# Loading rows 52 to 62 of each partition in six transfers instead of eight

## The chip, the cores and the metric

The kernel runs on one core of a Trainium2 chip. The metric is the time of one execution on the device in microseconds (us), less being better; runs of one kernel agree within about 0.2 us here. The core has a matrix engine (PE, TensorE), three engines for elementwise work and reductions (DVE is VectorE, ACT is ScalarE, POOL is GpSimd), a synchronizing engine (SP), and 16 DMA engines that move data between the device memory and the on-chip memory. On-chip memory has 128 partitions. PE writes its results into a separate accumulator memory, from which DVE or ACT must copy them before PE can read them as an operand.

## What is computed

A router: 16 x 512 = 8192 rows of 1024 numbers are multiplied by a 1024 x 8 weight matrix, and a softmax is taken over the 8 results of each row.

```python
def reference(x, router_weights):          # x: 16 x 512 x 1024, router_weights: 1024 x 8, float32
    logits = np.matmul(x, router_weights)
    exp_logits = np.exp(logits - np.max(logits, axis=-1, keepdims=True))
    return (exp_logits / np.sum(exp_logits, axis=-1, keepdims=True)).astype(np.float32)
```

The input is 33.6 MB, and the output only 0.26 MB.

## The kernel before

Each of the 128 partitions holds 64 of the 8192 rows, and "row j" below means row j of every partition: 128 rows of the input, 512 KB in the device memory. The whole input is kept on chip in bf16 (`x_all`, `xa` in the code), which is 256 KB for a row.

**The stream.** Rows 0 to 3 come first, as float32 in two transfers that SP issues (into `x_f32`), and ACT casts them. All other rows are loaded by POOL's queue, converted to bf16 by the transfer itself. The list `LOADS` (L40) says how many rows each transfer holds, from the first four rows on: thirteen entries of 4 (rows 0 to 51), three of 2 (52 to 57), five of 1 (58 to 62). Row 63, the last, comes in three pieces of its columns (`PIECES`, of 4, 2 and 2 blocks of 128 columns). POOL issues all of them at the start (L174 and L187), and they run one after the other. Every load has a semaphore of its own (`s_ld[i]`, `s_z[i]` for the pieces).

**How rows are released.** SP waits for each load in turn (L162) and then adds the load's number of rows to one semaphore, `s_in`. PE takes 1 from it ahead of each row (L218). So a row is released only when the whole transfer that it belongs to has landed. The pieces of row 63 are waited for by PE itself (L312).

**What is done for a row.** PE transposes the row's eight 128 x 128 blocks (`loop_turn`, L282): five into one accumulator bank (`ptv`), three into another (`pts`). DVE copies the five to `xTv` (L403), ACT the three to `xTs` (L355). Then PE multiplies the eight copied blocks by the weights (`multiply`, L269 in the trace), which gives the 8 logits of the 128 rows in `lg`. Banks and copies exist twice, for even and odd rows.

**PE's order.** A loop of two rows per trip: turn of the odd row, product of the even row before it, turn of the next even row, two filler matmuls on constant data (`spare<-filler`), product of the odd row. The last trip ends with the turn of row 62. Behind the loop PE waits for the copies of row 61 (its bank is used again), and then does: the transposes of the first piece of row 63 (L315, into `pts`), the product of row 61 (L261), the transposes of the two other pieces (into `ptv` and `extra`), the product of row 62, and the product of row 63 (L329).

**The softmax** is done for groups of 8 rows: on DVE maximum (`mx`), difference (`ex`), sum, reciprocal and scaling (`out_all`), and on ACT the exponential (`ev`, L344). The groups are rows 0 to 3 with an unused half, 4 to 11, and so on; the last is 52 to 59. Inside the loops of DVE and ACT its steps stand between the copies of the rows that follow. The last four rows, 60 to 63, are done with a maximum (`low`, L454) and an exponential (L348) each, and a common sum and scaling at the very end (L507 to L511).

**The order behind the loops**, which the last group of the softmax shares with the last rows, is written out:

- DVE: copy of row 60; maximum and difference of the group 52 to 59; copy of row 61; sum of the group; maximum of row 60; reciprocal of the group; copy of row 62; maximum of row 61; copies of the second and third piece (L460); maximum of rows 62 and 63; scaling of the group; sum, reciprocal and scaling of rows 60 to 63.
- ACT: copy of row 60; exponential of the group; copy of row 61; exponential of row 60; copy of row 62; copy of the first piece (L385); exponentials of rows 61, 62 and 63.

**Stores.** SP issues two: one for the groups up to row 51 (L165), after the first piece of row 63 has landed, and one for the rest (L167), after the last scaling.

Of the kernel before, what the change touches and what calls it, by code (L numbers as in the profile page):

```python
# [11 lines left out]
def kernel(  # L12
# [24 lines left out]

    LOADS = [4] * 13 + [2, 2, 2] + [1] * 5  # L40
    PIECES = [4, 2, 2]
    G, SKIP = 8, 4
    TRIPS = 31
# [5 lines left out]
    DONE = ends[-2]  # L49
    assert sum(LOADS) == J - 1 and sum(PIECES) == KO and ends[-1] == J - ALONE  # L50

# [6 lines left out]
    def sb(name, shape, dtype):  # L58
        size = mybir.dt.size(dtype)
        for n in shape[1:]:  # L60
            size *= n
        at = place[0]
        place[0] = -(-(at + size) // 64) * 64
        return nc.alloc_sbuf_tensor_at(name, shape, dtype, offset=at).ap()
# [5 lines left out]
    xa = sb("x_all", [P, J, D], bf16)  # L70
    x_f32 = sb("x_f32", [P, LOADS[0], D], fp32)
    identity = sb("identity", [P, P], bf16)
# [33 lines left out]
    s_w = nc.alloc_semaphore("s_w")  # L106
    s_ld = [sem(f"s_ld{i}") for i in range(len(LOADS))]
    s_z = [sem(f"s_z{i}") for i in range(len(PIECES))]
# [22 lines left out]

    first = [sum(LOADS[:i]) for i in range(len(LOADS))]
    cols = [sum(PIECES[:i]) for i in range(len(PIECES))]
# [21 lines left out]

    for j in range(LOADS[0]):
        sp.wait_ge(s_cast, j + 1)
        sp.sem_inc(s_in, 1)
    for i, r in enumerate(LOADS):
        if i:  # L160
# [383 lines left out]
```

## Time and profile before

| What | Value |
|---|---|
| Median of 4 runs | 86.60 us (86.49 to 86.69) |
| The profiled execution | 86.54 us |
| Its span, from the first to the last instruction | 85.08 us |
| Busy: PE, DVE, ACT, POOL | 62.6, 39.5, 37.9, 13.4 us |
| Granted clock of PE, mean (1 is full) | 0.987 |
| Input loads on POOL's queue, share of the 16 DMA engines over the span | 90.5% |
| Device memory read | 33.59 MB, 398 GB/s over the span |
| Issue of the last load by POOL | ends at 16.7 us |

The page shows the span in 40 slices of 2.1 us. The digits are tenths of a slice in which the engine was busy.

```profile
PE   0054859999495977949596895949597799999760
DVE  0021412684374442845265362736357257665662
ACT  0039683564253352535245262525336246545470
...
DMA  2999999898989999999999999999999999999920
```

The DMA engines are busy from the second slice to nearly the last, and PE has gaps until the last ten slices. In the timelines a line gives the start and the length in us, the engine, the line of the kernel, the operation and its tile (result <- operands), the number of instructions merged into it, and in brackets how long the engine sat idle before it and what ended that. "PEq L218" is PE's wait for a released row.

### The profile page before, as it was taken

Reading aid. Unit: us, or ns where it says so; the run is one execution under the profiler, and the core shown is the slowest. Engines: PE = TensorE matmul, PEld = TensorE weight load, DVE = VectorE, ACT = ScalarE, POOL = GpSimd, SP = SyncE. Lnnn points to the kernel's source line nnn. Section 1 sums busy time; section 2 is a strip of 40 time slices with the busy share of each in tenths; the row PEclk is TensorE's granted clock in tenths of the full one; section 3 lists DMA queues with packets and bytes.
Section 4 is the critical chain, followed back from the end, with each engine's and each line's share of the span. In section 5 each row is a group of like instructions: output and inputs, shape, how many; then the busy total and the mean of one; then the engine's idle time right before and its main releaser. Section 6 shows DMA issues by size and latency. Waiting matters only on the chain. (4 is left out here: it accounts for less than half of the span.)

```text
span 85.1 us, 2942 instructions
## 1 busy us (share of the span) xinstructions
PE 62.6 (74%) x1094; PEld 51.4 (60%) x1094; DVE 39.5 (46%) x114; ACT 37.9 (45%) x81; POOL 13.4 (16%) x30
## 2 busy tenths in 40 slices
PE   0054859999495977949596895949597799999760
PEld 0042748888374765838474673837476588777650
DVE  0021412684374442845265362736357257665662
ACT  0039683564253352535245262525336246545470
POOL 0489999800000000000000000000000000000000
PEclk9999999999999999999999999999999999999995
DMA  2999999898989999999999999999999999999920
GB/s 39 362 428 308 231 189 243 189 243 189 243 189 239 193 239 193 239 193 239 193 239 193 239 193 239 193 239 193 239 193 212 216 212 212 200 212 208 190 103 23
DMA packets 3904, 18.12 MB, mean 213 GB/s; under 512 B 568, under 2 KB 1080, under 8 KB 2112
## 3 DMA queue, kind: packets, MB, share of 16 engines
q0 software_dynamic: 3312, 15.73, 90.5%
q1 hardware_dynamic: 576, 2.36, 7.1%
q10 hardware_dynamic: 16, 0.03, 0.2%
HBM read 33.59 MB, written 0.26 MB: 398 GB/s over the span
## 5 line engine op out<-in xcount | busy, mean ns | idle before, releaser
L355 ACT COPY xTs<-pts 128x384 bf16<-128x384 bf16 x63 | 30.0, 476 | 37.4 <-PE pts L282 37.1
L403 DVE COPY xTv<-ptv 128x640 bf16<-128x640 bf16 x63 | 31.0, 492 | 32.9 <-PE ptv L282 30.4
L282 PE MATMUL ptv<-identity,x_all 128*128 128x128 bf16 x311 | 28.3, 222 | 13.7 <-PEq L218 12.4
L282 PEld LDWEIGHTS ptv<-identity,x_all 128*128 (+1 forms) x311 | 18.5, 98 | 15.1 <-issue 15.0
L282 PE MATMUL pts<-identity,x_all 128*128 128x128 bf16 x186 | 21.1, 224 | 0.0
L269 PEld LDWEIGHTS lg<-w_bf,xTv 128*128 128x128 bf16 x305 | 15.5, 97 | 7.4 <-issue 0.6
L269 PE MATMUL spare<-filler 128*128 128x512 bf16 x61 | 19.0, 393 | 0.4
L269 PE MATMUL lg<-w_bf,xTv 128*128 128x8 bf16 x305 | 16.6, 167 | 0.0
L282 PEld LDWEIGHTS pts<-identity,x_all 128*128 x186 | 13.4, 100 | 0.0
L269 PE MATMUL lg<-w_bf,xTs 128*128 128x8 bf16 x183 | 13.2, 166 | 0.0
L174 POOL DMA_DIRECT2D x_all<-in_x_dram x20 | 10.7, 607 | 2.8 <-POOLq L151 2.8
L269 PEld LDWEIGHTS lg<-w_bf,xTs 128*128 128x128 bf16 x183 | 8.9, 96 | 0.0
L269 PEld LDWEIGHTS spare<-filler 128*128 128x128 bf16 x61 | 4.3, 99 | 2.5 <-issue 2.5
L276 PE MATMUL lg<-ident,w 8*128 8x8 f32 x8 | 1.0, 251 | 5.3 <-PEq L274 5.3
L276 PEld LDWEIGHTS lg<-ident,w 8*128 8x128 f32 x8 | 0.9, 198 | 5.3 <-issue 5.3
L341 ACT CAST x_all<-x_f 128x1024 bf16<-128x1024 f32 x4 | 4.0, 1044 | 0.0
L423 DVE TENSOR_REDUCE mx<-lg 128x8 f32 x8 | 1.8, 225 | 4.4 <-DVEq L473 3.9
L341 ACT ACT_TABLE_LOAD x1 | 1.3, 1283 | 5.5 <-ACTq L339 5.5
L392 DVE CAST identity<-ident 128x128 bf16<-128x128 f32 x1 | 0.5, 518 | 5.2 <-POOL ident L180 5.2
L344 ACT ACTIVATE ev<-ex 128x64 f32<-128x64 f32 x8 | 2.0, 256 | 1.6 <-DVE ex L423 0.9
L439 DVE TENSOR_REDUCE ssum<-ev 128x8 f32<-128x64 f32 x8 | 1.8, 220 | 0.1
L187 POOL DMA_DIRECT2D x_all<-in_x_dram x3 | 1.7, 697 | 0.0
(41 smaller groups left out, 16.0 us busy)
## 6 DMA issues: line engine op xcount, KB each, us to landing
x_all<-in_x_dram POOLq DMA_DIRECT2D x12, 1024.0 KB, 32.1
x_f<-in_x_dram SPq DMA_DIRECT2D x2, 1024.0 KB, 6.3
x_all<-in_x_dram POOLq DMA_DIRECT2D x3, 512.0 KB, 59.9
x_all<-in_x_dram POOLq DMA_DIRECT2D x5, 256.0 KB, 64.1
out_dram<-out_all SPq DMA_DIRECT2D x1, 208.0 KB, 1.9
x_all<-in_x_dram POOLq DMA_DIRECT2D x1, 128.0 KB, 65.7
x_all<-in_x_dram POOLq DMA_DIRECT2D x2, 64.0 KB, 65.4
out_dram<-out_all SPq DMA_DIRECT2D x1, 48.0 KB, 1.5
```

The costliest lines, as they stand in the source:

```text
L174: nc.gpsimd.dma_start(out=xa[:, first[i]:first[i] + r, :], in_=x_rows[:, first[i]:first[i] + r, :]).then_inc(s_ld[i], 16)
L187: nc.gpsimd.dma_start(out=xa[:, J - 1, c], in_=x_rows[:, J - 1, c]).then_inc(s_z[i], 16)
L269: return pe.matmul(spare, lhsT=filler[:, 0:P], rhs=filler, start=True, stop=True)
L276: t = pe.transpose(w_ps[:, n, :], w8[:, :, n], ident[0:KO, 0:KO])
L282: turn_like = pe.transpose(turn_ap(0, 0), xa[:, 0, 0:P], identity).ins
L341: act.copy(xa[:, k, :], x_f32[:, k, :]).then_inc(s_cast, 1)
L344: return act.activation(ev, ex, func=Exp).then_inc(s_ev, 1)
L355: act.copy(xTs[j % 2], pts[j % 2][:, 0:SN, :]).then_inc(s_c[j % 2], 1)
L392: dve.tensor_copy(out=identity, in_=ident).then_inc(s_idb, 1)
L403: dve.tensor_copy(out=xTv[j % 2], in_=ptv[j % 2][:, 0:VN, :]).then_inc(s_c[j % 2], 1)
L423: return dve.add_instruction(kind(name=f"I-{nc.next_id()}", engine=dve.engine, **k))
L439: dve.reduce_sum(ssum[:, :, 0], ev, axis=X).then_inc(s_d, 1)
```

## The change

One line. `LOADS` gets a fourteenth entry of 4, one entry of 2 fewer and two of 1 fewer. Rows 52 to 55 come in one transfer, where there were two of two rows; rows 58 and 59 come in one, where there were two of one row. Rows 56 and 57 stay together, rows 60, 61 and 62 stay alone, and row 63 keeps its pieces.

```diff
-    LOADS = [4] * 13 + [2, 2, 2] + [1] * 5
+    LOADS = [4] * 14 + [2, 2] + [1] * 3
```

What follows from the list follows with it: two transfers and two semaphores fewer, two waits and increments fewer on SP, and increments of `s_in` by 4 (rows 52 to 55) and by 2 (rows 58 and 59) where they were by 2 and 2, and by 1 and 1. The programs of PE, DVE and ACT are the same, instruction by instruction.

## The prediction

> **What bounds the kernel now.** I read the chain of waits first, since it says what the end hangs on.
>
> ```profile
> 80.11 0.04 issue
> 80.16 0.44 PE ptv L282 x5
> 80.60 0.17 PE pts L282 x3
> 80.77 0.06 issue
> 80.82 0.38 PE pts L315 x4
> ...
> 81.97 0.35 PE lg L329 x8
> 82.33 0.02 issue
> 82.35 0.18 DVE low L454
> ```
>
> It begins at 80.11 us, with the turn (the eight transposes) of row 62; everything before is the stream. From 81.97, where the last row's product starts, to the end at 85.08 is a fixed run of small steps, so the question is what moves 81.97. The product waits for ACT's copy of the last row's first piece (81.24 to 81.825), and that copy waits for the piece's transposes at 80.82. Next, PE's timeline, rows 48 to 62 (a row begins at each "ptv L282"):
>
> ```profile
> 22.72 0.44 PE L282 MATMUL ptv<-identity,x_all 128*128 128x128 bf16 x5 [1.03 <-PEq L218]
> ...
> 61.65 0.44 PE L282 MATMUL ptv<-identity,x_all 128*128 128x128 bf16 x5 [1.05 <-PEq L218]
> ...
> 66.52 0.44 PE L282 MATMUL ptv<-identity,x_all 128*128 128x128 bf16 x5 [1.06 <-PEq L218]
> ...
> 67.81 0.44 PE L282 MATMUL ptv<-identity,x_all 128*128 128x128 bf16 x5
> ...
> 68.45 0.44 PE L282 MATMUL ptv<-identity,x_all 128*128 128x128 bf16 x5
> ...
> 69.53 0.44 PE L282 MATMUL ptv<-identity,x_all 128*128 128x128 bf16 x5
> ...
> 70.18 0.44 PE L282 MATMUL ptv<-identity,x_all 128*128 128x128 bf16 x5
> ...
> 72.99 0.44 PE L282 MATMUL ptv<-identity,x_all 128*128 128x128 bf16 x5
> ```
>
> A bracket marks a wait for data (L218): PE waits about 1.05 us after every load of four rows, and then runs without one from row 48 (66.52) to row 55 (72.99). The later waits are short, at rows 56 (73.89), 60 (77.67) and 62 (80.16). The DMA's share by stretch is 0.99 to 1.13 from 61 to 80 us, and the granted clock 1.00. So the load stream sets the pace, and PE touches it at row 62.
>
> Last, ACT's timeline at the end:
>
> ```profile
> 79.66 0.26 ACT L344 ACTIVATE ev<-ex 128x64 f32<-128x64 f32 x1 [0.86 <-DVE ex L423]
> 79.82 0.46 ACT L355 COPY xTs<-pts 128x384 bf16<-128x384 bf16 x1
> 80.27 0.27 ACT L348 ACTIVATE ev<-lg,low 128x8 f32<-128x8 f32 x1
> 80.80 0.48 ACT L355 COPY xTs<-pts 128x384 bf16<-128x384 bf16 x1 [0.27 <-PE pts L282]
> 81.24 0.58 ACT L385 COPY xTz<-pts 128x512 bf16<-128x512 bf16 x1
> ```
>
> It idles twice, 0.86 and 0.27 us; these gaps are the room that the softmax of the last group (rows 52 to 59) has now.
>
> **Part 1, the stream.** The trace's records of landings (last of the sixteen increments of each load) give 66.350 for rows 48 to 51, then 68.845, 71.283, 73.723 for the loads of two, 74.977, 76.265, 77.500, 78.737, 79.990 for those of one, and 80.685, 81.005, 81.337 for the pieces. A load of two takes 2.44 to 2.50 us, of one 1.24 to 1.29 (mean 1.253). A load of four takes 4.85 to 4.90: nine periods of PE's marks, 22.72 to 66.52, are 43.80, so 4.867 each. Rows 52 to 62 took 13.640. The new sizes need 4.867 + (2.44 to 2.50) + 2.44 + 3 x 1.253 = 13.51 to 13.57: row 62 and the pieces land 0.07 to 0.13 us earlier. A load of two against two of one is 2.44 against 2.51: 0.07 for each load saved, at most. The Trainium skill ("DMA: Bandwidth & Descriptors", the anatomy of one DMA on the gpsimd path) gives each DMA a fixed cost of about 2.0 us; paid in full, it would make two loads fewer worth 4 us, which the landings above don't show.
>
> POOL issues two loads fewer, about 0.61 us each, around 14 us; they land some 60 us after their issue, so the queue ahead of them hides this (uncovered it would be a gain of 1.2). SP has two waits and two increments fewer, 17 ns each, while it waits for data anyway, and its first store (80.70) goes with the first piece's landing, 0.1 earlier; the results that it needs besides, of rows up to 51, are written at 74.78 and about 1.2 later with the change, still before it. PE's, DVE's and ACT's programs are unchanged. All this I cost at nothing.
>
> **Part 2, rows 52 and 53 come later.** They were released at 68.85; now all four wait for the load that ends at 66.35 + 4.87 = 71.22. From landing to turn is 0.17 (66.350 to 66.52), so row 52 starts at 71.39 instead of 70.18: PE idles 1.2 us there. The Trainium skill ("Perfetto Trace Analysis", DMA Optimizations) speaks against the change here: splitting transfers may let work start sooner, if the DMA engines are mostly idle. They aren't in this stretch, though the effect on the start of row 52 is the one that it describes.
>
> **Part 3, does PE catch up?** The pattern after a wait is read from row 48: 1.29 to the next row (queue empty, fillers late), then 0.65 and 1.08 by turns. From row 48 to 55 that is 6.47. From row 52 to 62 it is 6.47 for seven rows, then 0.65 + 1.08 + 0.65 = 8.85. So row 60 starts at 71.39 + 7.12 = 78.51, row 61 at 79.59 and row 62 at 80.24. The data of row 60 and 62 are ready by 77.6 and 80.1, so PE doesn't wait again. Row 62 is 0.08 later than before, while the stream is done earlier: the end stops being paced by data.
>
> **Part 4, the softmax of rows 52 to 59 comes later still.** It needs row 59's product, which follows row 60's turn. That turn comes 0.84 later (78.51 for 77.67); the product follows 0.88 after an unbroken turn (70.18 to 71.06) instead of 1.09 (77.67 to 78.755), so it is 0.63 late: 79.385. I move the chain by 0.63: DVE's maximum 79.14 to 79.77, difference 80.03, ACT's exponential 79.655 to 80.285, copy of row 61 79.82 to 80.45 (its data are ready at 80.23), ending 80.91; row 60's exponential 80.27 to 80.90. What is queued behind on ACT? The copy of row 62, ready at 80.24 + 0.64 = 80.88, follows an exponential by 0.16 (79.655 to 79.817): 81.06. Then the copy of the piece: one instruction follows a copy by 0.37 (10.07 to 10.44 in ACT's start): 81.43, against 81.24.
>
> PE's side: the piece's transposes wait for row 61's copy, 80.91 + 0.07 = 80.98, end 81.36, so the data are ready at 81.40 and ACT is the later one. The product starts 0.73 after that copy (81.24 to 81.97): 82.16. DVE's copy of row 62 goes from about 80.96 behind row 61's sums, and the two small pieces end near 82.20; the fifth product, which needs the first of them, comes 0.10 after 82.16 and the seventh 0.15 after, so this has about 0.1 us of slack.
>
> **The sum.** 82.16 - 81.97 = +0.19 us. The profiled execution took 86.54, 85.08 of span and 1.46 around it; it becomes 86.73. The median of the runs, 86.60, is 0.06 above it, so 86.79: I say 86.8.
>
> **Bounds of what the trace doesn't show** (these queues with both gaps filled): below, if ACT takes the row 61 copy early and only row 62's turn holds the piece, the end moves by 0.08; above, if no ACT instruction overlaps the one before, 80.285 + 0.26 + 0.46 + 0.27 + 0.48 brings the piece's copy to 81.75, +0.51. ACT's rows show overlap of about 0.1 wherever two instructions meet, so I take a value near the lower end. The length of the four-row load adds -0.02 to +0.03.
>
> **Rivals.** (a) The end remains paced by the stream, and the gain of 0.07 to 0.13 is kept: 86.47 to 86.53. For it: the chain before begins at a data wait, and every later step follows the data. Against: 8.85 us of unbroken PE work has to fit between 71.22 and row 62's landing at 79.88. It decides if PE does two rows in under 1.67 instead of 1.73. (b) The delay is absorbed, 0 to 0.1: 86.6 to 86.7. For it: 0.86 us of ACT idle time before the group's exponential. Against: the copies' order on ACT is fixed, and the group arrives 0.63 late. (c) ACT and DVE back up further, at the upper bound: +0.4 to +0.5, 87.0 to 87.1. For it: row 62's copies wait on both engines; against: the overlaps seen. That the change does nothing is excluded by the program's order: one load of four more, one of two and two of one fewer.
>
> **How the numbers follow.** Forecast (0.08 to 0.3, most likely 0.19) 0.66; (a) 0.12; (b) 0.10; (c) 0.12. A measurement of this kernel tells about 0.2%, 0.17 us, from no change. Of the forecast some 0.48 lies above that and 0.18 below; with (c) slower is 0.60. Of (a) I give 0.06 to a larger saving per load, faster than 0.17; the rest, 0.06, with (b) and 0.18 makes same 0.34. The likeliest case alone is 86.65 to 86.95. For 8 in 10 I reach down to the upper edge of (a) and up to the lower edge of (c): 86.53 to 87.05.
>
> **What would show it.** In the changed profile: PE's data waits at row 52 of about 1.2 us (start near 71.4) and none after it to the end; row 62 near 80.24; DVE's last "mx" near 79.77; ACT without its 0.27 idle, the piece's copy near 81.43; the product at L329 near 82.16. I am wrong if a data wait still stands before row 62, if the piece's copy starts by 81.24, or if the rows after 52 run at another spacing than 0.65 and 1.08.

## The result, and the profile after

The changed kernel takes 86.79 us in the median (86.67 to 86.99, 52 runs), the kernel before 86.59 us (78 runs). The ratio is 1.0022 with a 95% interval of 1.0017 to 1.0027: slower by 0.19 us, small but clear of noise. The profiled execution took 86.72 us (before: 86.54), its span is 85.26 us (before: 85.08), and 1.46 us lie around it as before.

The chain of waits of the changed kernel (start in us, length, engine, tile and line):

```profile
71.36 0.04 issue
71.41 0.44 PE ptv L282 x5
...
79.56 0.20 PE lg L269 x8
79.76 0.02 issue
79.78 0.24 DVE mx L423
...
80.30 0.26 ACT ev L344
80.55 0.37 ACT xTs L355
80.92 0.26 ACT ev L348
81.18 0.37 ACT xTs L355
81.55 0.50 ACT xTz L385
82.04 0.14 issue
82.18 0.35 PE lg L329 x8
```

Before, the chain began at 80.11, at the turn of row 62, one step behind a landing. Now it begins at 71.36, at row 52, runs through unbroken PE work to row 59's product (79.56), and passes by DVE's maximum into five ACT instructions that touch each other. The end has changed hands: from the stream to PE, and then to ACT's queue.

PE's timeline of the changed kernel, at the starts of rows 48, 52, 53, 60, 61 and 62:

```profile
66.54 0.44 PE L282 MATMUL ptv<-identity,x_all 128*128 128x128 bf16 x5 [1.03 <-PEq L218]
...
71.41 0.44 PE L282 MATMUL ptv<-identity,x_all 128*128 128x128 bf16 x5 [1.06 <-PEq L218]
72.70 0.44 PE L282 MATMUL ptv<-identity,x_all 128*128 128x128 bf16 x5
...
78.52 0.44 PE L282 MATMUL ptv<-identity,x_all 128*128 128x128 bf16 x5
79.60 0.44 PE L282 MATMUL ptv<-identity,x_all 128*128 128x128 bf16 x5
80.25 0.44 PE L282 MATMUL ptv<-identity,x_all 128*128 128x128 bf16 x5
```

The bracket at 71.41 is the last data wait. Row 62's data landed at 79.948 and row 62 was turned at 80.25: the data lay ready. Before, row 62 still waited for its data (landed at 79.990):

```profile
80.16 0.44 PE L282 MATMUL ptv<-identity,x_all 128*128 128x128 bf16 x5 [0.41 <-PEq L218]
```

ACT's timeline at the end of the changed kernel:

```profile
80.30 0.26 ACT L344 ACTIVATE ev<-ex 128x64 f32<-128x64 f32 x1 [0.65 <-DVE ex L423]
80.46 0.46 ACT L355 COPY xTs<-pts 128x384 bf16<-128x384 bf16 x1
80.91 0.27 ACT L348 ACTIVATE ev<-lg,low 128x8 f32<-128x8 f32 x1
81.08 0.47 ACT L355 COPY xTs<-pts 128x384 bf16<-128x384 bf16 x1
81.44 0.60 ACT L385 COPY xTz<-pts 128x512 bf16<-128x512 bf16 x1
```

The idle 0.27 us ahead of row 62's copy is gone, and the piece's copy starts at 81.44 instead of 81.24. The first piece landed at 80.616, 0.07 earlier than before, and then waited 0.82 us for its copy instead of 0.56.

### The profile page after: what moved, and what is told of

The parts are those of the page before. It is cut to its first block, busy times and chain, and to the rows that moved or that the text cites. A ratio compares the mean times of both kernels' runs of the same rounds, so it can differ in the third digit from the quotient of the medians.

```text
span 85.3 us, 2938 instructions
## 1 busy us (share of the span) xinstructions
PE 62.8 (74%) x1094; PEld 51.7 (61%) x1094; DVE 39.3 (46%) x114; ACT 37.8 (44%) x81; POOL 12.4 (15%) x28
## 5 line engine op out<-in xcount | busy, mean ns | idle before, releaser
L269 PEld LDWEIGHTS lg<-w_bf,xTv 128*128 128x128 bf16 x305 | 15.5, 98 | 7.6 <-issue 0.8
L269 PE MATMUL spare<-filler 128*128 128x512 bf16 x61 | 19.2, 396 | 0.4
L269 PE MATMUL lg<-w_bf,xTv 128*128 128x8 bf16 x305 | 16.6, 167 | 0.0
L269 PE MATMUL lg<-w_bf,xTs 128*128 128x8 bf16 x183 | 13.2, 166 | 0.0
L174 POOL DMA_DIRECT2D x_all<-in_x_dram x18 | 9.7, 604 | 2.8 <-POOLq L151 2.8
L269 PEld LDWEIGHTS lg<-w_bf,xTs 128*128 128x128 bf16 x183 | 8.9, 96 | 0.0
L269 PEld LDWEIGHTS spare<-filler 128*128 128x128 bf16 x61 | 4.4, 101 | 2.3 <-issue 2.3
L423 DVE TENSOR_TENSOR ex<-lg,mx 128x64 f32<-128x64 f32 x8 | 1.7, 217 | 0.0
```

The lines of the kernel that those rows point to most:

```text
L174: nc.gpsimd.dma_start(out=xa[:, first[i]:first[i] + r, :], in_=x_rows[:, first[i]:first[i] + r, :]).then_inc(s_ld[i], 16)
L269: return pe.matmul(spare, lhsT=filler[:, 0:P], rhs=filler, start=True, stop=True)
L423: return dve.add_instruction(kind(name=f"I-{nc.next_id()}", engine=dve.engine, **k))
```

## The experiments

The theory: rows 52 to 55, released late, leave PE a backlog that it doesn't work off before row 62; the last group's softmax comes late by it, and ACT's queue behind its exponential holds the piece's copy. The rivals: the merge of rows 58 and 59 or the loads themselves cost the time; or row 62's slightly later turn alone does; or a late release costs time even when PE catches up.

The kernel before was timed beside each set, and its median was 86.58, 86.75, 86.77 and 86.72 us in the four sets. So kernels of different sets are compared by their ratio to it.

### One merge at a time

```diff
-    LOADS = [4] * 14 + [2, 2] + [1] * 3
+    LOADS = [4] * 14 + [2] + [1] * 5
```

> The merge of rows 52 to 55 alone; 58 and 59 stay single. Theory (PE's unbroken run from row 52 paces the end): row 52 at 71.4, PE unbroken to row 62, the same time as the change, 86.79, 0.2 above before. Rival (the merge of 58 and 59, or the stream, brings the loss): the time of before, 86.59.

Measured: 86.83 us against 86.58, ratio 1.0026 (1.0016 to 1.0036). The merge of rows 52 to 55 alone brings the whole loss.

```diff
-    LOADS = [4] * 14 + [2, 2] + [1] * 3
+    LOADS = [4] * 13 + [2, 2, 2, 2] + [1] * 3
```

> The merge of rows 58 and 59 alone; 52 to 55 stay two loads of two. Theory: row 58 waits for both, starts near 76.3 instead of 75.83, but row 62 is still paced by its data, near 80.1, and the last group's product is only 0.4 late, which ACT's gaps take up: 86.54 to 86.60, no loss. Rival (this merge brings the loss): 86.79.

Measured: 86.69 against 86.58, ratio 1.0011 (1.0003 to 1.0020), runs from 86.53 to 86.91. This is between the two expectations, and the theory's "no loss" is missed. PE's and ACT's timelines of this kernel (rows 58, 59 and 60, then the end of ACT's queue):

```profile
76.47 0.44 PE L282 MATMUL ptv<-identity,x_all 128*128 128x128 bf16 x5 [0.37 <-PEq L218]
77.80 0.44 PE L282 MATMUL ptv<-identity,x_all 128*128 128x128 bf16 x5
78.44 0.44 PE L282 MATMUL ptv<-identity,x_all 128*128 128x128 bf16 x5
```

```profile
80.22 0.26 ACT L344 ACTIVATE ev<-ex 128x64 f32<-128x64 f32 x1 [0.65 <-DVE ex L423]
80.38 0.46 ACT L355 COPY xTs<-pts 128x384 bf16<-128x384 bf16 x1
80.84 0.27 ACT L348 ACTIVATE ev<-lg,low 128x8 f32<-128x8 f32 x1
81.00 0.47 ACT L355 COPY xTs<-pts 128x384 bf16<-128x384 bf16 x1
81.36 0.60 ACT L385 COPY xTz<-pts 128x512 bf16<-128x512 bf16 x1
```

The bracket shows a data wait at row 58 that the kernel before didn't have (it turned row 58 at 75.83 without one). It puts a smaller backlog into the same place: the group's exponential is 0.45 us late, counted as in the table further down, and ACT's 0.27 us gap ahead of row 62's copy is used up. So the gaps don't take up the whole delay, though I had expected them to. The piece's copy follows its landing by 0.66 us instead of 0.56; that loses 0.10, and the earlier landing gives 0.09 back, so this execution ends 0.02 later by that table. Of the 0.15 us by which its profiled time (86.69) lies above that of the kernel before (86.54), 0.11 arose ahead of the landing of rows 48 to 51 (66.464 against 66.350), which both kernels load alike. So the table supports a loss of about 0.02 from this merge; what makes the rest of the 0.1 us between the medians stays open. The two losses don't add up either: both merges together cost no more than the first alone.

### A larger dose

```diff
-    LOADS = [4] * 14 + [2, 2] + [1] * 3
+    LOADS = [4] * 15 + [1] * 3
```

> A larger dose: fifteen loads of four, so that rows 56 to 59 come in one too, then 60, 61, 62 alone. Theory: row 56 starts near 76.27 instead of 75.07, PE runs unbroken from there with 1.29 for the first row, row 62 near 81.67, everything behind it moves with it: 1.42 above the change, 88.2. Rival (the stream paces the end and one load fewer helps it): 86.5 to 86.8.

Measured: 88.26 (88.15 to 88.32), ratio 1.0192 (1.0179 to 1.0206). PE's timeline at rows 52, 56, 57 and 62:

```profile
71.47 0.44 PE L282 MATMUL ptv<-identity,x_all 128*128 128x128 bf16 x5 [1.06 <-PEq L218]
...
76.40 0.44 PE L282 MATMUL ptv<-identity,x_all 128*128 128x128 bf16 x5 [1.13 <-PEq L218]
77.69 0.44 PE L282 MATMUL ptv<-identity,x_all 128*128 128x128 bf16 x5
...
81.79 0.38 PE L282 MATMUL ptv<-identity,x_all 128*128 128x128 bf16 x4
```

From a wait at row 56 PE has six rows left, and takes 5.39 us for them with no gap, while the data of row 62 had landed at 79.92. The release of rows 56 to 59 sets the end here as that of rows 52 to 55 does in the change, and the loss follows the dose: the ratios put this kernel 1.47 us above the change, where 1.42 was worked out.

### The queue behind the group's exponential

In the changed kernel the exponential of the group goes behind the piece's copy on ACT, and the sum and reciprocal go with it on DVE.

```diff
     act_copy(J - 4, 0)
-    act.wait_ge(s_ex, 1)
-    power()
     act_copy(J - 3, 1)
...
     act.copy(xTz[0], z_bank[0]).then_inc(s_zc[0], 1)
+    act.wait_ge(s_ex, 1)
+    power()
...
     dve_copy(J - 3, 1)
-    dve.wait_ge(s_ev, 1)
-    total()
     low_alone(0)
-    recip()
     dve_copy(J - 2, 2)
...
     low_alone(2)
+    dve.wait_ge(s_ev, 1)
+    total()
+    recip()
     low_alone(3)
```

> The changed kernel with the exponential, sum and reciprocal of the group 52 to 59 put behind the copies of rows 61, 62 and the first piece on ACT and DVE. Theory (ACT's queue behind that exponential sets the end): the piece's copy starts near 81.31 instead of 81.44, 0.13 earlier, 86.65. Rival (row 62's later start, 80.25 for 80.16, or the stream sets the end): no difference from the change, 86.79.

Measured: 86.66 against 86.58, ratio 1.0009 (1.0000 to 1.0018). ACT's timeline at the copies of row 61, row 62 and the piece:

```profile
80.34 0.48 ACT L355 COPY xTs<-pts 128x384 bf16<-128x384 bf16 x1 [0.60 <-PE pts L282]
80.86 0.27 ACT L348 ACTIVATE ev<-lg,low 128x8 f32<-128x8 f32 x1
81.03 0.47 ACT L355 COPY xTs<-pts 128x384 bf16<-128x384 bf16 x1
81.38 0.60 ACT L383 COPY xTz<-pts 128x512 bf16<-128x512 bf16 x1
...
81.86 0.28 ACT L344 ACTIVATE ev<-ex 128x64 f32<-128x64 f32 x1
```

PE's order and the loads are those of the change, and the larger part of the loss is gone: ACT's queue was the last link. The edit moves two steps of DVE as well, but the product starts 0.14 us behind the end of ACT's copy of the piece in the change (82.04 to 82.18) and 0.15 here (81.98 to 82.13), as it did before (0.14): ACT's copy is what it waits for. PE's backlog is still there, with row 62 turned 0.30 us after its data landed (80.34, 80.042), and this goes with the part of the loss that is left. The same order in the kernel before:

> The kernel before with the group's exponential, sum and reciprocal behind the last copies, as in the third experiment. Theory: before has gaps on ACT and is paced by the landing of the first piece, so the other order brings nothing: 86.55 to 86.62 where before is 86.58, ratio 0.9995 to 1.0005. Rival (the order is worth its 0.13 in any kernel, and the gain of both remedies came from it): ratio 0.9985.

Measured: ratio 1.0000 (0.9992 to 1.0009). There the piece's copy waits for its data, and the order has nothing to give.

### PE's backlog

The first attempt takes one of the two fillers (L269, `spare<-filler`) out of each trip of PE's loop, in the changed kernel and in the one before:

```diff
     with nc.body("rows_multiply", valid_engines=only_pe):
         fill()
-        fill()
         multiply(1, None)
```

> The changed kernel with one filler matmul per two rows instead of two (0.215 us less PE work per two rows). Theory: PE catches up with the stream before row 62, which waits for its data again and starts near 80.12; the earlier stream shows, 0.05 to 0.1 below before, 86.50 to 86.55. Rival (PE's pace is not the cause): 0.2 above before, as the change. If the granted clock falls without the filler, both this and its twin are slower.

> The kernel before with one filler per two rows. Theory: it waits for data at row 62 already, so PE's saved time brings nothing: 86.55 to 86.62. Rival (PE's work counts in the end of both): about 0.2 or more below before.

Measured: the changed kernel with one filler takes 87.00 (86.44 to 87.59) against 86.75, ratio 1.0022 (0.9991 to 1.0052), in two heaps: six runs of 86.44 to 86.62 and six of 87.39 to 87.59. The kernel before with one filler keeps its time, 1.0007 (0.9998 to 1.0015). The profile of the changed one is from the upper heap. Its stretches of 4 us (busy time of PE, its weight loads, DVE, ACT and POOL, then the granted clock, the DMA's share and GB/s):

```profile
68.00:72.00 4.00, 2.61 (x58) 2.42 (x55) 1.48 (x3) 1.44 (x3) 0.00 (x0) 1.00 0.99 204
72.00:76.00 4.00, 3.96 (x65) 3.47 (x63) 2.27 (x7) 1.73 (x5) 0.00 (x0) 0.67 1.05 209
76.00:80.00 4.00, 4.00 (x80) 3.63 (x77) 2.35 (x8) 2.36 (x5) 0.00 (x0) 0.90 1.13 207
```

The clock falls to 0.67 just while PE works off the backlog. So this run says nothing clean about the backlog. The lower heap (middle 86.53) lies 0.22 us below the kernel before of its set, on the side that was expected but further than the 0.05 to 0.1, and no profile of it was taken. What it shows is the fillers' work: with two of them the clock stands at 1.00 through all of this stretch.

The second attempt leaves out only the three pairs behind the turns of rows 52, 54 and 56, by running the loop's body in three loops (26 trips, 3 without fillers, 2 with them):

```diff
-        pe.br_lt(r_x[0], left_of(TRIPS - 1), on_true="rows_multiply", on_false="rows_done")
+        pe.br_lt(r_x[0], left_of(26 - 1), on_true="rows_multiply", on_false="late_multiply")
+    with nc.body("late_multiply", valid_engines=only_pe):
+        multiply(1, None)
+        pe.br("late_turn")
...
+        pe.br_lt(r_x[0], left_of(29 - 1), on_true="late_multiply", on_false="last_multiply")
+    with nc.body("last_multiply", valid_engines=only_pe):
+        fill()
+        fill()
+        multiply(1, None)
...
```

> The changed kernel without the pairs of filler matmuls that follow the turns of rows 52, 54 and 56 (up to 1.29 us less PE work; all other fillers stay, so that the clock should hold). Theory (PE's backlog from row 52 sets the end): PE catches up and waits for data at row 58 and at row 62; row 60 starts near 78.28 instead of 78.52, the product of row 63 near 81.94 instead of 82.18: 0.24 below the change, 86.5 to 86.6 where before is 86.58. Rival (a late release costs time even when PE catches up, or the loads themselves do): 86.75 to 86.8.

> The kernel before without the same fillers. Theory: its PE waits for data at rows 60 and 62 in any case, so the time stays, 86.55 to 86.62. Rival (PE's work counts at the end of both kernels alike): 0.2 below before.

Measured: the changed kernel 1.0002 (0.9993 to 1.0011), the kernel before 0.9997 (0.9988 to 1.0006). With the clock held (mean 0.993), less PE work takes the whole loss away from the one and gives the other nothing. PE's timeline of the first at rows 52, 53, 58 and 60:

```profile
71.54 0.44 PE L282 MATMUL ptv<-identity,x_all 128*128 128x128 bf16 x5 [1.06 <-PEq L218]
72.36 0.44 PE L282 MATMUL ptv<-identity,x_all 128*128 128x128 bf16 x5
...
76.44 0.49 PE L282 MATMUL ptv<-identity,x_all 128*128 128x128 bf16 x5
...
78.38 0.44 PE L282 MATMUL ptv<-identity,x_all 128*128 128x128 bf16 x5
```

Row 52 is as late as in the change, yet row 60 comes 6.84 us behind it instead of 7.11. PE has caught up: row 58 starts 0.17 us behind the landing of its data (76.268), and row 62 (80.20) 0.17 behind its own (80.035), the distance from landing to turn where PE waits. So when PE catches up the late release makes no net loss against the kernel before. It isn't free: the group's exponential is still 0.40 us late in this execution, and the piece's copy follows its landing by 0.65 us instead of 0.56; the earlier landing of the piece pays for that (table below). Does that depend on the other merge? The kernel with the merge of rows 52 to 55 alone, without the three pairs (the order behind the loops is that of the change):

> The merge of rows 52 to 55 alone (58 and 59 single) without the fillers after rows 52, 54, 56. Theory: PE catches up before row 60 as in the kernel with both merges, row 62 waits for its data, near the time of before, ratio 0.9990 to 1.0003. Rival (what the missing fillers recover depends on the merge of 58 and 59): 1.0015 or more.

Measured: 1.0003 (0.9994 to 1.0012). It doesn't, and with rows 58 and 59 apart the group's exponential is only 0.11 us late.

### Both remedies

> The changed kernel with both: the group's exponential behind the last copies, and no fillers after rows 52, 54, 56. Theory: either alone takes the delay away, so together they end where the data allow, 0.05 to 0.1 below before through the earlier stream: 86.48 to 86.55. If the two gains added up it would be 86.42.

Measured: 86.71 against 86.77, ratio 0.9988 (0.9979 to 0.9997). It is the only kernel here whose interval lies below the one before, by 0.06 us in the medians, and that interval ends just short of 1. The third experiment's order brought nothing in the kernel before, and neither did the missing fillers, so what is gained is the stream's. The traces' starts differ by up to 0.3 us between executions; counted from the landing of rows 48 to 51, which all these kernels load alike, the records give (us):

| Kernel | Group's exponential | First piece lands | Its copy starts | Row 63's product |
|---|---|---|---|---|
| before | 13.31 | 14.34 | 14.89 | 15.62 |
| the change | 13.93 | 14.25 | 15.07 | 15.81 |
| 52 to 55 alone | 13.93 | 14.25 | 15.07 | 15.81 |
| 58 and 59 alone | 13.76 | 14.24 | 14.90 | 15.64 |
| fifteen fours | 15.42 | 14.21 | 16.56 | 17.30 |
| change, exponential later | 15.40 | 14.23 | 14.92 | 15.66 |
| change, fewer late fillers | 13.71 | 14.19 | 14.85 | 15.59 |
| before, fewer late fillers | 13.46 | 14.30 | 14.86 | 15.59 |
| change, both remedies | 15.24 | 14.20 | 14.76 | 15.49 |
| before, exponential later | 15.36 | 14.32 | 14.88 | 15.61 |
| 52 to 55 alone, fewer late fillers | 13.42 | 14.24 | 14.84 | 15.57 |

Where data set the end, the copy follows the landing by 0.56 us (before, before with either remedy, and the change with both); in the change it is 0.82. The piece lands 0.09 to 0.15 us earlier in every kernel with fewer loads, and only with both remedies is all of it kept.

## Why the prediction was right

- **The stream's gain** (part 1). Rows 52 to 62 took 13.577 us, just above the 13.51 to 13.57 that was worked out, against 13.640 before; in other executions with these loads they took 13.53 to 13.58. The gain was there, 0.06 us, and paid nothing, as predicted, since nothing waited for it.
- **Row 52** (part 2) started at 71.41, predicted 71.39. The size of PE's wait was wrong: I wrote 1.2 us, the difference of two row starts, and the profile has 1.06. The wait is counted from the end of the last matmul before, and the pipelined matmuls of the row before end later (70.35) than the next row would have started (70.20). No later number used it.
- **PE's catching up** (part 3). Row 60 came at 78.52 (78.51), row 61 at 79.60 (79.59), row 62 at 80.25 (80.24). The spacings read off rows 48 to 55 held for ten rows, and no data wait came back. The dose of fifteen fours repeated them.
- **The softmax's delay** (part 4). The maximum came at 79.78 (79.77), the exponential at 80.30 (80.285), row 62's copy at 81.08 (81.06), the piece's copy at 81.44 (81.43), the product at 82.18 (82.16). Moving the group's exponential out of the way took most of the loss away, and shortening PE's backlog all of it.
- **The sum**, +0.19, met both the profiled executions (86.72 against 86.54, +0.18) and the medians (+0.20).
- **The rivals.** The stream as the pace of the end (a) fell by its own condition: PE was to do two rows in under 1.67 us, and kept to 1.73. The 1.67 was a little too strict: row 62 came 0.13 us behind the start that its landing allowed, over five pairs of rows, so about 1.70 would have done. With three pairs of fillers away PE met the condition, but the gain was used up on ACT (1.0002); it was kept only with both remedies (0.9988). The absorbed delay (b) fell in the change, and is what happens in part when rows 58 and 59 are merged alone. Queues without overlap (c) weren't seen: ACT's instructions still overlap by about 0.1 us.

The experiments correct one point of the theory: ACT's gaps were not as good a cushion as I took them for in the second experiment.

## What to carry to other kernels

Near the end of this stream, the size of a load wasn't only its price on the DMA engines: it set how late its rows were released, and the work of all rows after it had then to fit, unbroken, into what the stream had left. In another kernel, work that out from the spacing of rows in a stretch without waits, here 8.85 us for ten rows against 8.71 us from their release (71.24) to the landing of row 62 (79.95). Then look at what is interleaved with the last rows on the other engines: a group's work that was in their gaps may be the link that holds the end.

## What the runs showed of the hardware

One filler of 0.215 us fewer per two rows was enough to make the granted clock fall to half for stretches of 3.41 us, or two of them on end, again and again; the mean of the span went from 0.99 to between 0.87 and 0.92. From 30 us on, PE's longest wait for data was 1.4 us in those profiles, against 1.1 with both fillers. The Trainium skill ("TensorE: Matmul & The Clock Gate", Part 1) has the clock fall after an idle window of about 3.4 us; the stretches have that length here, but in this part of the profiles PE was never idle for as long as one. The changed kernel's time split into two heaps 0.9 us apart, and the kernel before, with the same dips (0.57 in the stretch from 68 to 72 us of its profile), did not. That the heaps come from where a dip falls against the release of rows 52 to 55 is argued from one profile, not shown; the mean clock doesn't separate them (0.873 to 0.916 in the lower heap, 0.881 to 0.901 in the upper). Three pairs fewer in the last 15 us left the clock at 0.99.
